# Output projection: sums of weights stand beside kept pieces of the first group, and transpositions move one piece back

## The chip, the cores and the metric

One core of a Trainium2 chip runs the whole program. The metric is the device time of one execution in microseconds (us). Three runs of the kernel before gave 922.68, 921.38 and 921.91 us, a median of 921.91 us. The profiled execution took 922.59 us by its own measurement, of which the profile's span covers 920.8 us.

## The reference, cut to what matters

Two layers act on a sequence of 256 rows of width 2048. Each layer projects its input, runs three groups of attention heads, gates their outputs, and maps the joined result through one output projection. A residual and a layer norm close the layer.

```
for l in range(DEPTH):                       # DEPTH = 2
    h = x @ w_in                             # x (256, 2048)
    ...
    mkv = mem @ w_mem_kv                     # memory keys and values, mem (256, 2048)
    ...
    y = concat([y_a * silu(a_z), y_b * silu(b_z), y_m * silu(m_z)])   # (256, 2048)
    out = y @ w_out                          # (256, 2048) x (2048, 2048)
    x = layer_norm(ALPHA * x + out, ln_g, ln_b)
```

The change is in `y @ w_out`, for columns 0 to 1023 of it, and in how the next layer's input is transposed after the layer norm.

## The kernel before, in words

**Pieces.** Weights come from memory as pieces of 512 KB (128 partitions x 1024 floats). `plan()` lists all of them in the order of use, and `take()` hands them out. For each piece SP issues a DMA into a tile `raw` (a ring of four). ACT casts it to a short-mantissa tile `wh` (L256, ring of four). DVE subtracts to get the rest `wl` (L263, ring of three). PE multiplies with both: an operand's high part with `wh`, its low part with `wh`, its high part with `wl`. `advance` keeps the high tile three pieces ahead and the low tile two ahead. PE and SP run in the order in which the program is written. DVE and ACT run in an order that a scheduler works out before the kernel is built, and each then works through its queue strictly in that order.

**The output projection.** Columns 0 to 1023 are two groups of 512 columns (n = 0 and n = 1), columns 1024 to 2047 are two more. The first two groups are computed by a Strassen-like scheme (`out_unit`, L872) for the first 3 (layer 0) or 2 (layer 1) of the four k-quarters of y, and plainly for the rest. The letters of `OUT_B` and `OUT_A` set the row of pieces:

- B, a plain block product of one quarter: 6 matmuls on 512 columns (`plain`, L882).
- K, a kept piece: the quarters that the scheme leaves out. A piece feeds both row tiles, t = 0 and 1, so 12 matmuls (`kept`, L898). Those of n = 1 come first, then those of n = 0.
- T, a sum of weight blocks, which DVE adds (L255) before ACT and DVE split it: 6 matmuls (`sums`, L912).
- O, a piece of the last two column groups, 12 matmuls (`others`, L1126). What the row leaves of them follows at its end.

A row is `OUT_B[l]`, then `OUT_A[l]`. With 3 O at the end of layer 0's row (one of `OUT_A`'s letters TO and two more) and 1 at the end of layer 1's, the last T stands three pieces and one piece before the end.

**Banks.** PSUM has eight banks, here 0 to 7. `pair()` alternates between banks 0-1 and 2-3 at each call; every stream of pieces that needs two banks calls it when it starts. Banks 4 to 7 serve the head generators, and then `out_unit`: before the change bank 7 collects (t 0, n 0), 6 (t 0, n 1), 5 (t 1, n 0) and 4 (t 1, n 1); when T starts, 7 and 6 are read into the residual (L913, L914) and used again for two of the four sums. After the last T eight DVE instructions (L922 to L929) combine the banks into the residual `res`, and three `bn_stats` (L931) follow.

**After the row.** In layer 0 the generator `norm_between` (L794) runs beside layer 1's first 16 pieces (the memory's keys and values, L965): one `tick()` per piece lets it go on. It aggregates the statistics (L799), takes the reciprocal root (L496 to L501, ACT's square root with a load of its table), normalises `res` in eight instructions (L804), and after `yield 3` transposes it in eight steps of four transpositions (L817) into banks 4 and 5 in turn, which ACT reads (L820). When the 16 pieces are done, the next stream of pieces (`ws_pieces(..., first=4)`, L1011) writes banks 4 and 5. In layer 1 eight closing pieces (`last3`, numbered 0 to 7 here) follow the row, the last five of which have tiles of their own (`room`, `w`). They run twice: for row tile 0 (L1141 on), then for row tile 1. Then comes the last norm.

Of the kernel before, what the change touches and what calls it, by code (L numbers as in the profile page):

```python
# [18 lines left out]
T = 256  # L19
# [9 lines left out]
PART_B = "WB" * 12  # L29
PART_A = "TW" * 16  # L30
QUARTERS = (3, 2)
OUT_B = ("BBOBBOBKBKBKBKB", "BBKBKBKBKBKKKK")
OUT_A = ("TO" * 12 + "OO", "TO" * 8)

G_MK, G_MV, G_BQK, G_AQ0, G_AK0, G_AQ1, G_AK1, G_MQ, G_BZ, G_AZ0, G_AZ1, G_MZ, G_WO = range(13)
HI_AHEAD, LO_AHEAD, RAWS = 3, 2, 4
# [16 lines left out]
def hybrid_trunk_kernel(  # L53
# [87 lines left out]
    def plan():  # L141
        for l in range(L):
            def keys(p):
                g = w512[l, G_MK].rearrange("(h q) p n -> q p h n", h=2)
                return Load(g[p // 2, :, :, p % 2 * 512:p % 2 * 512 + 512], (2, 512))

            def add_sums(b11, b12, b21, b22, n, beside):
                sums = []
                for q in range(len(b11)):
                    for k, d in enumerate(Load(None, (2, n)) for _ in range(4)):  # L150
                        d.sum = (q, k)
                        d.parts = [[(0, b11[q]), (1, b12[q])], [(2, b22[q])], [], [(3, b21[q])]][k]
                        sums.append(d)
                for d in sums:
                    d.at = len(loads)
                    if d.sum[0] and d.sum[1] < 2:
                        i = d.sum[0] * 4 - 4
                        d.behind = (sums[i + 2].at, sums[i + 1].at) if d.sum[1] == 0 else (sums[i + 3].at, sums[i + 2].at)
                    if d.sum[1] < 2:
                        early.append(d)  # L160
                    loads.extend((d, next(beside)))

            def group(g, kp, n):
                loads.extend(Load(g[i], (kp, n)) for i in range(16 // kp))

            for p in range(8):
                if p % 2 == 0:
                    loads.append(Load(memT[p // 2], (4, T), "res" if l == 0 else None, (memq[l], p // 2)))
                loads.append(Load(w512[l, G_MV, p], (2, 512)))
                if p:  # L170
                    loads.append(keys(p - 1))
            loads.append(keys(7))
            for p in range(8):
                if l == 0 and p < 4:
                    loads.append(Load(xT[p], (4, T), "res", (xq[l], p)))
                if p == 4:
                    break
                loads.append(Load(w512[l, G_BQK, p], (4, 256)))
            stream = iter([Load(w512[l, g, p], (4, 256)) for g in (G_BQK, G_AQ0, G_AK0, G_AQ1) for p in range(8)][4:])
            b11, b12, b21, b22 = ([w388[l, n, 2 * q + k] for q in range(4)] for k, n in ((0, 0), (0, 1), (1, 0), (1, 1)))  # L180
            plain = iter([Load(b, (2, 388)) for b in b11 + b22 + b21])
            loads.extend(next(stream if c == "W" else plain) for c in PART_B)
            add_sums(b11, b12, b21, b22, 388, stream)
            group(w388[l, 2], 2, 388)
            loads.extend(stream)
            group(w388[l, 3], 2, 388)
            for g in (G_AK1, G_MQ, G_BZ, G_AZ0, G_AZ1, G_MZ):
                loads.extend(Load(w512[l, g, p], (4, 256)) for p in range(8))
            u, kq = [w512[l, G_WO + n] for n in range(2)], QUARTERS[l]
            b11, b12, b21, b22 = ([u[n][2 * q + k] for q in range(kq)] for k, n in ((0, 0), (0, 1), (1, 0), (1, 1)))  # L190
            last3 = [w256[l].rearrange("h q p n -> q p h n")[p // 2, :, :, p % 2 * 512:p % 2 * 512 + 512] for p in range(8)]
            plain = iter([Load(b, (2, 512)) for b in b11 + b22 + b21])
            kept = iter([Load(u[n][p], (2, 512)) for n in (1, 0) for p in range(2 * kq, 8)])
            others = iter([Load(w512[l, G_WO + 2, p], (2, 512)) for p in range(8)] +
                          ([] if l == L - 1 else [Load(b, (2, 512)) for b in last3]))
            loads.extend(next(dict(B=plain, K=kept, O=others)[c]) for c in OUT_B[l])
            add_sums(b11, b12, b21, b22, 512, others)
            loads.extend(others)
            if l == L - 1:
                for p, b in enumerate(last3):  # L200
                    home = ("asv", "mk", "mv", "qk", "qk")[p - 3] if p >= 3 else None
                    loads.append(Load(b, (2, 512), home))
                    if home:
                        loads[-1].room = p
# [589 lines left out]
    def norm_between(l, x):  # L794

        mvt = small([P, 2, 2], "mvt")
        rstd = small([P, 2], "rstd")
        for t in range(2):
            dve.bn_aggr(mvt[:, t], stats[:, t, :4])  # L799
        rsqrt(rstd, mvt[:, :, 1], 2, LN_EPS)  # L800
        for q in range(4):
            for t in range(2):
                r = res[:, t, columns(q)]
                dve.tensor_scalar(r, r, mvt[:, t, 0:1], rstd[:, t:t + 1], op0=ALU.subtract, op1=ALU.mult)  # L804
            if q == 0:
                yield 2
        yield 3
        for q in range(4):
            o = operand()
            x.append(o)  # L810
            for j in range(0, 4, 2):
                pt, = yield from banks(1)
                z = gated()
                for jj in range(2):
                    kt = q * 4 + j + jj
                    for t in range(2):
                        pe.transpose(ps[:, pt, jj * T + t * P:jj * T + (t + 1) * P], res[:, t, kt * P:(kt + 1) * P], ident)  # L817
                for jj in range(2):
                    kt = q * 4 + j + jj
                    act.activation(z[:, jj], ps[:, pt, jj * T:(jj + 1) * T], AF.Identity, bias=lnt[:, 1, kt:kt + 1], scale=lnt[:, 0, kt:kt + 1])  # L820
                release(pt)
                parts(o[:, j:j + 2, 0], o[:, j:j + 2, 1], z)
                if j == 0:
                    z0 = z
                else:
                    x_differences(l, q, z0, z)
                yield 2 if (q, j) == (2, 2) else 1
# [44 lines left out]
    def out_unit(yq, ydiff, kq, rows):  # L872
        r11, r12, r21, r22 = (res[:, t, columns(n)] for t in range(2) for n in range(2))
        tmp = hd.tile([P, 512], F32, name=nm("tmp"), tag="term")
        open_ = set()

        def first(b):
# [3 lines left out]

        def plain():  # L882
            for q in range(kq):
                quarter(ps[:, 7], block(yq[q], 0, 0), first(7), False)
                if q == kq - 1:
                    act.copy(tmp, ps[:, 7])
                tick()
                yield
            for q in range(kq):
                quarter(ps[:, 6], ydiff[q][3], first(6), False)  # L890
                tick()
                yield
            for q in range(kq):
                quarter(ps[:, 7], block(yq[q], 0, 1), False, False)
                tick()
                yield

        def kept():  # L898
            for n in (1, 0):
                for p in range(2 * kq, 8):  # L900
                    w = take()
                    for kk in range(2):
                        kt = p * 2 + kk
                        for t, b in enumerate((7 - n, 5 - n)):
                            moving(ps[:, b], t, [v[:, kk] for v in w], yq[kt // 4], kt % 4, first(b), kt == 15)
                    if n and p == 7:
                        dve.scalar_tensor_tensor(r22, r22, ALPHA, ps[:, 4], op0=ALU.mult, op1=ALU.add)
                        open_.remove(4)
                    tick()
                    yield  # L910

        def sums():  # L912
            add_residual(0, columns(0), ps[:, 7], 0)  # L913
            dve.scalar_tensor_tensor(r12, r12, ALPHA, ps[:, 6], op0=ALU.mult, op1=ALU.add)  # L914
            open_.difference_update((6, 7))
            for q in range(kq):
                s1, s2, s3, s4 = ydiff[q]
                for b, a in ((4, s1), (6, s3), (7, s2), (5, block(yq[q], 1, 1))):
                    quarter(ps[:, b], a, first(b), q == kq - 1)
                    if q == kq - 1 and b == 5:  # L920
                        q5, q7, q6, q4 = (ps[:, b] for b in (4, 6, 7, 5))
                        dve.tensor_tensor(tmp, q6, tmp, op=ALU.subtract)  # L922
                        dve.scalar_tensor_tensor(r21, r21, ALPHA, tmp, op0=ALU.mult, op1=ALU.subtract)
                        dve.tensor_tensor(r21, r21, q7, op=ALU.add)
# [325 lines left out]
```

## Time and profile before

| | |
|---|---|
| median of 3 runs | 921.91 us (921.38 to 922.68) |
| profiled execution | 922.59 us, of which the span is 920.8 us |
| DVE busy | 720.0 us, 78% |
| ACT busy | 553.8 us, 60% |
| DMA | 196.21 MB, mean 213 GB/s |
| layer 0's row of the output projection | from 369.26 us to 452.44 us of the span |
| layer 1's row | ends, and the closing pieces begin, a little over 30 us before the span's end |

In rows of the timeline the columns are: start in us, duration in us, engine, line, operation, output<-input, shape, count, and in brackets the idle time before it with what ended that wait. Adjacent instructions of a kind are merged into one row. `PEld` is the loading of the stationary operand, which runs under the matmuls. Matmuls overlap, so the time of one is the distance between starts and not the duration shown.

### The profile page before, as it was taken

How to read it: one execution, taken by the hardware profiler on the slowest of the kernel's cores; microseconds unless marked ns; L12 is line 12 of the kernel's file. 1: busy time of each engine (PE TensorE's matmuls, PEld its weight loads, DVE VectorE, ACT ScalarE, POOL GpSimd, SP SyncE). 2: the span in 40 equal slices, each digit the busy share in tenths (PEclk: the TensorE clock that was granted, in tenths of full speed). 3: DMA queues.
4: the chain of work that ended last, by engine and by line, in shares of the span. 5: the costliest groups of instructions: out<-in, count | busy, mean ns of one | idle time of the engine just before them, and what ended most of it. 6: DMA issues, size and time to landing. Idle time of an engine off the chain costs nothing.

```text
span 920.8 us, 14554 instructions
## 1 busy us (share of the span) xinstructions
PE 908.2 (99%) x5480; PEld 795.6 (86%) x5480; DVE 720.0 (78%) x997; ACT 553.8 (60%) x809; POOL 13.5 (1%) x32
## 2 busy tenths in 40 slices
PE   8999999999999999999999999999999999999997
PEld 6889999998888888888878899999988888888875
DVE  6697788698665777799978768886877788777897
ACT  6565555676486766554568555557657676465550
POOL 1000000000000000000000000000000000100000
PEclk9999999999999999999999999999999999999998
DMA  8868786775444455886765687655644555868652
GB/s 300 279 204 275 253 282 204 235 242 177 158 138 160 161 177 189 300 271 221 232 209 173 200 293 252 224 192 175 225 159 137 196 175 179 288 214 294 215 173 92
DMA packets 65014, 196.21 MB, mean 213 GB/s; under 512 B 7088, under 2 KB 10288, under 8 KB 64944
## 3 DMA queue, kind: packets, MB, share of 16 engines
q1 hardware_dynamic: 63632, 192.55, 63.0%
q0 software_dynamic: 1024, 2.21, 0.7%
q8 instruction: 43, 0.70, 0.3%
q10 hardware_dynamic: 288, 0.52, 0.2%
q14 instruction: 27, 0.22, 0.1%
HBM read 193.16 MB, written 2.10 MB: 212 GB/s over the span
## 4 chain that ended last, share of the span: by engine, by line
PE 91%; DMA 3%; ACT 2%; DVE 2%; issue 1%; SPq 0%; ACTq 0%; DVEq 0%
PE ps L86 89%; DMA raw<-w 2%; DVE wl L263 1%; ACT wh L256 1%; PE ps L721 0%; DMA gws<-gate_w 0%; PE ps L817 0%; PE ps L759 0%; DVE w L263 0%; ACT sq L676 0%; SPq L344 0%; PE ps L688 0%; ACT sc L712 0%; SPq L339 0%; ACT res L861 0%
## 5 line engine op out<-in xcount | busy, mean ns | idle before, releaser
L263 DVE TENSOR_TENSOR wl<-raw,wh 128x1024 fp32r<-128x1024 f32 (+1 forms) x313 | 364.9, 1169 | 119.0 <-PE ps L86 59.8
L256 ACT CAST wh<-raw 128x1024 fp32r<-128x1024 f32 (+1 forms) x313 | 314.8, 1008 | 233.7 <-PE ps L86 130.8
L86 PE MATMUL ps<-x,wh 128*128 128x512 f32 x1408 | 446.4, 398 | 0.0
L86 PEld LDWEIGHTS ps<-x,wl 128*128 128x128 f32 x1408 | 265.1, 188 | 63.3 <-DVE wl L263 1.0
L86 PE MATMUL ps<-x,wl 128*128 128x256 f32 x1408 | 278.1, 279 | 0.3 <-DVE wl L263 0.3
L86 PE MATMUL ps<-wh,x 128*128 128x512 f32 (+1 forms) x852 | 246.3, 370 | 0.6 <-ACT wh L350 0.6
L86 PEld LDWEIGHTS ps<-x,wh 128*128 128x128 f32 x1408 | 219.6, 189 | 1.7 <-issue 0.3
L86 PEld LDWEIGHTS ps<-wh,x 128*128 128x128 f32 x852 | 155.0, 188 | 20.0 <-ACT wh L350 1.7
L86 PE MATMUL ps<-wl,x 128*128 128x512 f32 (+1 forms) x426 | 157.7, 370 | 0.0
L86 PEld LDWEIGHTS ps<-wl,x 128*128 128x128 f32 x426 | 80.0, 188 | 11.4 <-DVE wl L351 1.1
L256 ACT CAST wh<-term 128x776 fp32r<-128x776 f32 (+1 forms) x39 | 36.0, 923 | 49.4 <-DVE term L255 41.3
L263 DVE TENSOR_TENSOR wl<-term,wh 128x776 fp32r<-128x776 f32 (+1 forms) x39 | 41.5, 1065 | 16.6 <-PE ps L86 15.8
L255 DVE TENSOR_TENSOR term<-term,term 128x776 f32<-128x776 f32 (+1 forms) x39 | 41.3, 1060 | 0.7 <-DMA term<-w 0.7
L86 PE MATMUL ps<-wh,s 128*128 128x512 f32 (+1 forms) x144 | 41.2, 368 | 0.0
L86 PEld LDWEIGHTS ps<-wh,s 128*128 128x128 f32 x144 | 25.9, 188 | 3.2
L86 PE MATMUL ps<-wl,s 128*128 128x512 f32 (+1 forms) x72 | 26.6, 369 | 0.0
L712 ACT ACTIVATE sc<-sc,mx 128x128 f32<-128x128 f32 (+1 forms) x32 | 14.2, 444 | 7.5 <-DVE mx L710 7.4
L487 DVE SCALAR_TENSOR_TENSOR sz<-ps,sz 128x512 f32<-128x512 f32 x24 | 16.4, 686 | 2.8 <-ACT sz L486 2.1
L86 PE MATMUL ps<-wh,sc 128*128 128x388 f32 x64 | 16.5, 338 | 0.0
L86 PE MATMUL ps<-w,x 128*128 128x512 f32 (+1 forms) x72 | 15.0, 361 | 1.3 <-DVE w L263 1.2
L86 PEld LDWEIGHTS ps<-w,x 128*128 128x128 f32 x72 | 11.8, 189 | 4.4 <-DVE w L263 2.5
L491 DVE TENSOR_TENSOR s<-raw,s 128x512 fp32r<-128x512 f32 (+1 forms) x23 | 12.6, 569 | 3.1 <-ACT s L490 3.1
(221 smaller groups left out, 713.8 us busy)
## 6 DMA issues: line engine op xcount, KB each, us to landing
raw<-w SPq DMA_DIRECT2D x252, 512.0 KB, 4.3
raw<-w SPq DMA_DIRECT2D x64, 388.0 KB, 3.7
term<-w SPq DMA_DIRECT2D x24, 388.0 KB, 4.3
term<-w SPq DMA_DIRECT2D x15, 512.0 KB, 4.7
bias<-relw SPq DMA_DIRECT2D x16, 192.0 KB, 3.8
res<-xT SPq DMA_DIRECT2D x4, 512.0 KB, 6.3
res<-xn SPq DMA_DIRECT2D x4, 512.0 KB, 4.7
raw<-memT SPq DMA_DIRECT2D x4, 512.0 KB, 4.5
```

Of the source, the lines that this page charges most:

```text
L86: pe.matmul(o, l, r, start=start, stop=stop, skip_group_check=True)
L255: in_order(dve.tensor_tensor(d.raw, d.raw, d.plus, op=ALU.add))
L256: act.copy(d.hi, d.raw)
L263: in_order(dve.tensor_tensor(d.lo, d.raw, d.hi.bitcast(F32), op=ALU.subtract))
L487: dve.scalar_tensor_tensor(dst, a, scale, dst, op0=ALU.mult, op1=ALU.add)
L491: dve.tensor_tensor(lo, src, hi.bitcast(F32), op=ALU.subtract)
L712: act.activation(s[:, own[t]], s[:, own[t]], AF.Exp, bias=mx[:, t:t + 1], accum_out=zs[:, t:t + 1])
```

## The change

Three things change. First, the rows of letters: two K of layer 0 and four K of layer 1 (those of n = 0) move from `OUT_B` into `OUT_A`, beside T; as many O move to the row's end, so that 4 O (layer 0) and 5 O (layer 1) follow the last T. `add_sums` takes the row as a pattern for that. Second, the banks: (t 0, n 0) goes to a bank of its own, `x0`, and (t 1, n 1) to `x0 + 1`. They come from a further call of `pair()` ahead of O's own, so O of the same layer takes the other pair than before. Banks 4 and 7 are then untouched until T uses them. Third, `yield 3` before the transpositions becomes `yield 4`. The numbers of matmuls, sums and loads stay.

```diff
-OUT_B = ("BBOBBOBKBKBKBKB", "BBKBKBKBKBKKKK")
-OUT_A = ("TO" * 12 + "OO", "TO" * 8)
+OUT_B = ("BBOBBOBKBKBBOB", "BBKBKBKBKB")
+OUT_A = ("TKTK" + "TO" * 10 + "OOO", "TK" * 4 + "TO" * 4 + "OOOO")
...
-            def add_sums(b11, b12, b21, b22, n, beside):
+            def add_sums(b11, b12, b21, b22, n, pattern, beside):
...
-                for d in sums:
+                left = iter(sums)
+                for c in pattern:
+                    if c != "T":
+                        loads.append(next(beside[c]))
+                        continue
+                    d = next(left)
...
-                    loads.extend((d, next(beside)))
+                    loads.append(d)
...
-            add_sums(b11, b12, b21, b22, 388, stream)
+            add_sums(b11, b12, b21, b22, 388, PART_A, dict(W=stream))
...
-            loads.extend(next(dict(B=plain, K=kept, O=others)[c]) for c in OUT_B[l])
-            add_sums(b11, b12, b21, b22, 512, others)
-            loads.extend(others)
+            beside = dict(B=plain, K=kept, O=others)
+            loads.extend(next(beside[c]) for c in OUT_B[l])
+            add_sums(b11, b12, b21, b22, 512, OUT_A[l], beside)
...
-        yield 3
+        yield 4
...
         tmp = hd.tile([P, 512], F32, name=nm("tmp"), tag="term")
+        x0 = pair()
...
-                quarter(ps[:, 7], block(yq[q], 0, 0), first(7), False)
+                quarter(ps[:, x0], block(yq[q], 0, 0), first(x0), False)
...
-                        for t, b in enumerate((7 - n, 5 - n)):
+                        for t, b in enumerate((6, x0 + 1) if n else (x0, 5)):
...
-                    if n and p == 7:
-                        dve.scalar_tensor_tensor(r22, r22, ALPHA, ps[:, 4], op0=ALU.mult, op1=ALU.add)
-                        open_.remove(4)
+                    if p == 7 and n:
+                        dve.scalar_tensor_tensor(r22, r22, ALPHA, ps[:, x0 + 1], op0=ALU.mult, op1=ALU.add)
+                    elif p == 7:
+                        add_residual(0, columns(0), ps[:, x0], 0)
...
         def sums():
-            add_residual(0, columns(0), ps[:, 7], 0)
             dve.scalar_tensor_tensor(r12, r12, ALPHA, ps[:, 6], op0=ALU.mult, op1=ALU.add)
-            open_.difference_update((6, 7))
+            open_.remove(6)
...
-                for b, a in ((4, s1), (6, s3), (7, s2), (5, block(yq[q], 1, 1))):
+                for b, a in ((4, s1), (7, s3), (6, s2), (5, block(yq[q], 1, 1))):
```

How the order moves, at three places. Lines of the changed kernel are 5 or 6 higher than those of before. Numbers in names tell tiles apart.

**First place.** PE at layer 0's first O piece (operand `x_2901`, weights `wh_3711`, `wl_3743`), the third piece of the row, with what a row waits for, before:

```order
L86 MATMUL ps<-wl_3713,x_3654 128x512
L86 MATMUL ps<-wh_3711,x_2901 128x512 [waits Activation_49]
L86 MATMUL ps<-wh_3711,x_2901 128x512
L86 MATMUL ps<-wl_3743,x_2901 128x512 [waits DVE_49]
L86 MATMUL ps<-wh_3711,x_2901 128x512 x2
```

And in the changed kernel:

```order
L86 MATMUL ps<-wl_3713,x_3654 128x512
L86 MATMUL ps<-wh_3711,x_2901 128x512 [waits DVE_49]
L86 MATMUL ps<-wh_3711,x_2901 128x512
L86 MATMUL ps<-wl_3743,x_2901 128x512
L86 MATMUL ps<-wh_3711,x_2901 128x512 x2
```

The O piece's first matmul waited for ACT's cast, and its third for DVE's rest. It now waits for DVE at the first, and that covers the third: O writes the pair of banks that the last gate product filled, which DVE reads in L487 behind the rests of two pieces.

**Second place.** ACT in layer 1, at the readings of the last two steps of transpositions (rows with `sz<-ps,lnt`), just before the stream of pieces that writes banks 4 and 5; `wh_4859` is the cast of that stream's third piece, `mv` that of the memory's values, `s` and `sc` those of differences that DVE makes. Before:

```order
L256 CAST wh_4837<-raw_4748 128x1024
L490 CAST sc_4725<-raw_4727 128x256
L490 CAST mv_4384<-ps 128x1024
L490 CAST sc_4726<-raw_4727 128x256
L820 ACTIVATE sz_4785<-ps,lnt 128x256 x2
L490 CAST s_762_4724<-raw_4727 128x512
L820 ACTIVATE sz_4814<-ps,lnt 128x256 x2
L256 CAST wh_4859<-raw_4766 128x1024
```

In the changed kernel:

```order
L495 CAST sc_4749<-raw_4751 128x256
L495 CAST sc_4750<-raw_4751 128x256
L261 CAST wh_4814<-raw_4725 128x1024
L495 CAST mv_4384<-ps 128x1024
L825 ACTIVATE sz_4805<-ps,lnt 128x256 x2
L495 CAST s_768_4748<-raw_4751 128x512
L495 CAST x_4804<-sz_4805 128x2x256
L261 CAST wh_4859<-raw_4766 128x1024
L825 ACTIVATE sz_4836<-ps,lnt 128x256 x2
```

The last reading stood ahead of the cast `wh_4859` and stands behind it and behind the cast `x_4804` now.

**Third place.** DVE at the end of layer 1's row; `wl_8555` and `wl_8575` are the rests of closing pieces 1 and 2, `w_...` those of the pieces from 3 on. Before:

```order
L263 TENSOR_TENSOR wl_8555<-raw_8479,wh_8528 128x1024
L925 TENSOR_TENSOR res<-res,ps 128x512
L927 TENSOR_TENSOR res<-res,tmp_8086 128x512
L928 TENSOR_TENSOR res<-res,tmp_8086 128x512
L781 SCALAR_TENSOR_TENSOR res<-res,ps 128x512
L263 TENSOR_TENSOR wl_8575<-raw_8497,wh_8553 128x1024
L263 TENSOR_TENSOR w_8573<-room_8499,w_8573 128x1024
L781 SCALAR_TENSOR_TENSOR res<-res,ps 128x512
L263 TENSOR_TENSOR w_8584<-room_8499,w_8583 128x1024
L931 BN_STATS stats<-res 128x6 x2
L929 TENSOR_TENSOR res<-res,ps 128x512
L263 TENSOR_TENSOR w_8594<-raw_8502,w_8593 128x1024
```

In the changed kernel, where `wl_8496` and `wl_8519` belong to the last two O pieces and `wl_8537` to closing piece 0:

```order
L931 TENSOR_TENSOR res<-res,ps 128x512
L933 TENSOR_TENSOR res<-res,tmp_8092 128x512
L934 TENSOR_TENSOR res<-res,tmp_8092 128x512
L268 TENSOR_TENSOR wl_8496<-raw_8425,wh_8476 128x1024
L937 BN_STATS stats<-res 128x6 x2
L935 TENSOR_TENSOR res<-res,ps 128x512
L268 TENSOR_TENSOR wl_8519<-raw_8437,wh_8494 128x1024
L939 TENSOR_TENSOR res<-res,sc_8073 128x512
L937 BN_STATS stats<-res 128x6
L268 TENSOR_TENSOR wl_8537<-raw_8455,wh_8517 128x1024
L939 TENSOR_TENSOR res<-res,sc_8077 128x512
L268 TENSOR_TENSOR wl_8555<-raw_8480,wh_8535 128x1024
```

The steps that close the scheme stood among the rests of the closing pieces 1 to 5, and stand ahead of closing piece 1 now. ACT's casts there, before:

```order
L256 CAST wh_8510<-raw_8450 128x1024
L256 CAST wh_8528<-raw_8479 128x1024
L256 CAST wh_8553<-raw_8497 128x1024
L256 CAST w_8573<-room_8499 128x1024
L256 CAST w_8583<-room_8499 128x1024
```

In the changed kernel:

```order
L261 CAST wh_8517<-raw_8455 128x1024
L261 CAST wh_8535<-raw_8480 128x1024
L261 CAST w_8573<-room_8500 128x1024
L261 CAST wh_8553<-raw_8498 128x1024
L261 CAST w_8583<-room_8500 128x1024
```

The cast of closing piece 3 (`w_8573`) has come ahead of that of piece 2 (`wh_8553`).

More of the change, by code (lines that the diff above doesn't have):

```diff
@@ L883, in plain @@
             for q in range(kq):
-                quarter(ps[:, 7], block(yq[q], 0, 0), first(7), False)
+                quarter(ps[:, x0], block(yq[q], 0, 0), first(x0), False)
                 if q == kq - 1:
-                    act.copy(tmp, ps[:, 7])
+                    act.copy(tmp, ps[:, x0])
                 tick()
@@ L893, in plain @@
             for q in range(kq):
-                quarter(ps[:, 7], block(yq[q], 0, 1), False, False)
+                quarter(ps[:, x0], block(yq[q], 0, 1), False, False)
                 tick()
@@ L912, in sums @@
         def sums():
-            add_residual(0, columns(0), ps[:, 7], 0)
             dve.scalar_tensor_tensor(r12, r12, ALPHA, ps[:, 6], op0=ALU.mult, op1=ALU.add)
-            open_.difference_update((6, 7))
+            open_.remove(6)
             for q in range(kq):
                 s1, s2, s3, s4 = ydiff[q]
-                for b, a in ((4, s1), (6, s3), (7, s2), (5, block(yq[q], 1, 1))):
+                for b, a in ((4, s1), (7, s3), (6, s2), (5, block(yq[q], 1, 1))):
                     quarter(ps[:, b], a, first(b), q == kq - 1)
                     if q == kq - 1 and b == 5:
-                        q5, q7, q6, q4 = (ps[:, b] for b in (4, 6, 7, 5))
+                        q5, q7, q6, q4 = (ps[:, b] for b in (4, 7, 6, 5))
                         dve.tensor_tensor(tmp, q6, tmp, op=ALU.subtract)
```

## The prediction

> **What bounds the kernel now.** I began with the page: the busy times of the engines.
>
> ```profile
> span 920.8 us, 14554 instructions
> PE 908.2 (99%) x5480; PEld 795.6 (86%) x5480; DVE 720.0 (78%) x997; ACT 553.8 (60%) x809; POOL 13.5 (1%) x32
> ```
>
> PE is busy for all but 12.6 us of 920.8, and the change leaves the number of matmuls alone. So a gain can only come out of PE's idle time and out of matmuls that run slower than they need to. The next view is PE's timeline, for the pace of an undisturbed stretch.
>
> ```profile
> 397.90 0.62 PE L86 MATMUL ps<-wh,s 128*128 128x512 f32 x2
> ...
> 457.88 0.62 PE L86 MATMUL ps<-x,wh 128*128 128x512 f32 x2
> ```
>
> Between these starts lie 59.98 us and 264 matmuls on 512 columns: 0.227 us each. So a B or T piece takes 6 x 0.227 = 1.36 us, a K or O piece 2.72 us. Whatever takes longer is loss. I then walked PE's timeline through the places that the diff touches: layer 0's row, layer 1's first pieces (the transpositions), and layer 1's row with the closing pieces. Two of them show loss. The first is the boundary between the layers:
>
> ```profile
> 468.66 0.39 PE L86 MATMUL ps<-wl,x 128*128 128x512 f32 x1
> 470.71 1.00 PE L817 MATMUL ps<-ident,res 128*128 128x128 f32 x4 [1.66 <-DVE res L804]
> ...
> 475.90 0.60 PE L817 MATMUL ps<-ident,res 128*128 128x128 f32 x4
> 476.26 0.72 PE L86 MATMUL ps<-wh,x 128*128 128x512 f32 x2
> ...
> 479.13 0.60 PE L817 MATMUL ps<-ident,res 128*128 128x128 f32 x4
> 479.48 0.71 PE L86 MATMUL ps<-x,wh 128*128 128x512 f32 x2
> ```
>
> PE stood for 1.66 us before the first transposition step. The piece behind it started at 471.47 and took until 475.90, against 479.13 - 476.26 = 2.87 us for the next one. The windows say why (us, PE busy, granted clock, DMA share, GB/s):
>
> ```profile
> 473.00:474.00 1.00, 1.00 (x5) 0.50 0.03 12
> 474.00:475.00 1.00, 1.00 (x5) 0.50 0.00 0
> 476.00:477.00 1.00, 1.00 (x8) 1.00 0.68 188
> ```
>
> After the idle time PE was granted half its clock for some 3 us. The second place is the closing pieces of row tile 0:
>
> ```profile
> 888.14 0.61 PE L86 MATMUL ps<-wh,x 128*128 128x512 f32 x2
> ...
> 889.77 3.51 PE L86 MATMUL ps<-w,x 128*128 128x512 f32 x14
> 894.53 4.29 PE L86 MATMUL ps<-w,x 128*128 128x512 f32 x16 [1.25 <-DVE w L263]
> ...
> 902.74 7.22 PE L86 MATMUL ps<-w,x 128*128 128x512 f32 x42
> ```
>
> From 888.14 to 902.74 run 54 matmuls in 14.60 us; at 0.227 they take 12.26. The loss is 2.3 us, half of it the wait of 1.25 for a rest of DVE.
>
> **The change, part by part.** Durations are those of the profiled execution, 922.59 us, which lies 0.7 above the median of 921.91; the sum is made against it.
>
> *Transpositions one piece later.* The end of the normalisation sets when the first step may start:
>
> ```profile
> 461.15 0.26 DVE L799 BATCH_NORM_AGGREGATE mvt<-stats 128x2 f32<-128x24 f32 x1
> 468.59 1.22 DVE L263 TENSOR_TENSOR wl<-raw,wh 128x1024 fp32r<-128x1024 f32 x1 [1.26 <-ACT wh L256]
> 470.11 3.74 DVE L804 TENSOR_SCALAR res<-res,mvt,rstd 128x512 f32<-128x512 f32 x8
> ```
>
> The statistics were aggregated at 461.15, but the eight normalisations came at 470.11, behind a rest that had itself waited. A block takes 3.74 / 8 = 0.47 us, so the first is ready at 470.6. After the change PE runs one more memory piece before the first step: 468.89 (its last matmul's start at 468.66 and 0.23) + 2.8 = 471.7. Even with DVE's chain unmoved the wait is gone, with 1 us to spare, and with it the cause of the half clock. And the chain should come earlier, since the scheme's last combinations are now done before layer 0's last four pieces rather than three. From the end of the piece at 468.89 to the start of the next memory piece but one at 476.26 the trace has 7.37 us; undisturbed it is a step (479.48 - 479.13 = 0.35), a piece (2.88) and a step, 3.59. The term is **-3.8 us**. What is late next is the other end of the transpositions, below.
>
> [...]
>
> *O takes the other pair of banks.* Layer 0's first O writes the pair of the last gate product:
>
> ```profile
> 370.23 0.60 ACT L486 ACTIVATE sz<-ps 128x512 f32<-128x512 f32 x1
> 372.01 0.61 PE L86 MATMUL ps<-wh,x 128*128 128x512 f32 x2
> 372.05 0.69 DVE L487 SCALAR_TENSOR_TENSOR sz<-ps,sz 128x512 f32<-128x512 f32 x1
> ```
>
> The matmul at 372.01 began while DVE was just starting its read of that pair. It must now wait until the read is done: 372.74 - 372.01 = **+0.7 us**. Bounds 0.4 (if DVE takes the read a little sooner, the O piece being one that needs its rest later) and 0.9 (if it starts 0.2 later). PE loses it whole, as every matmul behind it is in order. Layer 1 has no O before its first T, so it isn't paid there.
>
> *The last transposition step and the banks 4 and 5.* The stream behind the memory pieces writes these banks. It began at 504.21, two memory pieces behind the last step; after the change only one lies between. What must fit in it is ACT's reading of the last step:
>
> ```profile
> 498.20 0.60 PE L817 MATMUL ps<-ident,res 128*128 128x128 f32 x4
> 498.56 0.71 PE L86 MATMUL ps<-x,wh 128*128 128x512 f32 x2
> ...
> 504.21 0.63 PE L86 MATMUL ps<-x,wh 128*128 128x512 f32 x2
> ```
>
> ```profile
> 490.76 1.05 ACT L256 CAST wh<-raw 128x1024 fp32r<-128x1024 f32 x1 [3.02 <-DMA raw<-w]
> ...
> 499.60 1.02 ACT L490 CAST mv<-ps 128x1024 fp32r<-128x1024 f32 x1
> ...
> 500.81 1.03 ACT L820 ACTIVATE sz<-ps,lnt 128x256 f32<-128x256 f32 x2
> 501.72 0.63 ACT L490 CAST s<-raw 128x512 fp32r<-128x512 f32 x1
> 502.23 1.04 ACT L820 ACTIVATE sz<-ps,lnt 128x256 f32<-128x256 f32 x2
> 503.14 1.07 ACT L256 CAST wh<-raw 128x1024 fp32r<-128x1024 f32 x1
> ```
>
> The step ended at 498.56 and its reading at 503.27: 4.7 us later, with 5.65 of cover. In the new order the reading stands behind one more cast of 1024 columns and one of an operand. Walk ACT's queue from the end of memory piece 13, which was 498.20 here: the `mv` cast starts 1.40 later, takes 0.90 to the next, the second last reading 0.91, `s` 0.51, the operand 0.52, `wh` 0.95, the last reading 1.04; together 6.23. With the small `sc` cast (0.31) and a DVE step for the operand (0.4) it is 6.9. PE is there after a step, a piece, a step and a piece: 0.35 + 2.88 + 0.35 + 2.79 = 6.37. That leaves 0.6; the walk counts no idle time of ACT, so I take **+0.8 us**. The low bound is 0: ACT's lag goes back to its wait of 3.02 us for a load, and that need not recur. The high bound takes the old lag whole: 4.7 + 0.95 - 2.83 = 2.8. I stay near the low end because the queue's rows, added up, lie there.
>
> *The closing pieces.* The losses from 888 to 903 come from this order on DVE and ACT:
>
> ```profile
> 884.38 1.05 ACT L256 CAST wh<-raw 128x1024 fp32r<-128x1024 f32 x1 [2.01 <-DMA raw<-w]
> 885.63 1.05 ACT L256 CAST w<-room 128x1024 fp32r<-128x1024 f32 x1 [0.20 <-DMA room<-w]
> ...
> 892.67 0.67 DVE L929 TENSOR_TENSOR res<-res,ps 128x512 f32<-128x512 f32 x1
> 893.25 1.22 DVE L263 TENSOR_TENSOR w<-raw,w 128x1024 fp32r<-128x1024 f32 x1
> ```
>
> The rest that PE waited for at 894.53 ran at 893.25 behind the scheme's last combinations. With five O behind the last T these are over before closing piece 1, so DVE's part of the loss goes. What remains is ACT, which takes its casts as loads land, and piece 3's now stands ahead of piece 2's: if that load is late, piece 2 waits. A whole recovery is -2.3; losing 1.3 more than that leaves -1.0. I take **-1.6 us**, the middle, as neither end has a nearer row.
>
> *Kept pieces beside sums, in both rows.* A sum costs DVE an addition and a rest:
>
> ```profile
> 418.56 1.22 DVE L263 TENSOR_TENSOR wl<-term,wh 128x1024 fp32r<-128x1024 f32 x1 [0.58 <-PE ps L86]
> ```
>
> DVE waits here 0.58 us per T and wide piece, on PE, so it keeps up with a wide piece beside each T; K and O are equally wide, so T beside K costs PE nothing. Before T, B and O now alternate where B and K did: also the same widths. The reads of the first banks (0.7 us of DVE in the place of the same read elsewhere) fit into that slack; uncovered they would cost up to 0.7 each. **0**.
>
> Sum: -3.8 + 0.7 + 0.8 - 1.6 = -3.9, so 918.7 for an execution like the profiled one, and 918.0 for the median.
>
> **The rivals.** *All covered.* The bank wait vanishes, the first O's is at its low bound, and the tail comes back whole: -3.8 + 0.4 - 2.3 = -5.7, 916.3. For it speaks the load wait of 3.02 that need not recur; against it that the first O's wait shows in the rows almost by itself.
>
> *The tail is not recovered.* The inverted casts cost what DVE gives back: -3.8 + 0.7 + 0.8 = -2.3, 919.6. For it: the casts at 884.38 and 885.63 both waited for loads. Against: more lead from five O.
>
> *The wait moves to the banks, and with it the half clock.* The reading has its old lag, PE waits 2.8 in the place of 0.8, and then runs at half clock, which cost 7.37 - 3.59 - 1.66 = 2.1 at the boundary: -3.9 + 2.0 + 2.1 = +0.2, 922.1. For it: 1.66 of waiting had this effect at 470.71. Against: a wait of 1.25 at 894.53 had not, by the pace of the 16 matmuls behind it (4.13 us for 16, 0.26 each, not 0.45). [...]
>
> *Slower.* ACT may lag more than at the last step. At the sixth step it did:
>
> ```profile
> 488.81 0.60 PE L817 MATMUL ps<-ident,res 128*128 128x128 f32 x4
> ...
> 495.98 1.01 ACT L820 ACTIVATE sz<-ps,lnt 128x256 f32<-128x256 f32 x2
> ```
>
> The step ended at 489.16 and its reading at 496.99, 7.8 later, after that load came late. With this lag the bank wait is 7.8 - 2.9 = 4.9, and 0.95 for the cast now ahead, 5.9 in the place of 0.8, and 2.1 of half clock: -3.9 + 5.1 + 2.1 = +3.3, 925.2. It turns the sign when the bank wait passes 2.6: 3.9 + 0.8 = 4.7 are saved without it, less 2.1 for the clock. For it: loads near 490 are late already. Against: six us of queue lie between, in which ACT caught up to 4.7.
>
> *The change doesn't do what it says.* The waiting goes, but the half clock stays, because something other than the wait brought it about: -3.9 + 2.1 = -1.8, 920.1. For it: a wait of 1.25 did not halve the pace. Against: the clock is 1.00 again a few us later, and no other loss lies near.
>
> **How the numbers follow.** Times of rivals are against the median, 921.9. Forecast (916.6 to 919.6) 0.57; all covered 0.12; tail not recovered 0.08; half clock stays 0.04; bank wait with half clock 0.12; slower 0.07. A measurement of this kernel tells about 0.2%, 1.8 us, from no change: faster means under 920.07, slower over 923.75. So faster is 0.57 + 0.12 + 0.08 = 0.77, same 0.04 + 0.12 = 0.16, slower 0.07. The range runs from 915.6 (all covered, and the first O's wait gone too, with 0.3 left for rows that I cost at nothing) to 922.1 (bank wait at its upper bound, with half clock); beyond it lie the slower case and some 0.08 of the ends.
>
> **What would show it.** No idle time before the first transposition and a granted clock of 1.00 through 480; the memory piece behind it at 2.88. A wait for DVE of 0.4 to 0.9 at the first O near 372. A wait for ACT of 0 to 2.8 before the stream behind the memory pieces, near 500. From closing piece 2 to the run of 42 matmuls 12.3 to 13.6 us in the place of 14.60, with the wait, if any, on ACT. Wrong it would be if the clock dropped at a new place, if T beside K left PE waiting for DVE in the rows, or if more than 3 us were lost at banks 4 and 5.

## The result and the profile after

The changed kernel takes 919.28 us (median of 7 runs, 918.70 to 921.25); the kernel before, in 7 runs beside it, 922.68. The ratio is 0.9964, with a 95% interval of 0.9952 to 0.9976: faster by 0.36%, clear of no change. The forecast was 918.0 against 921.9, 0.42%. The profiled execution took 919.35 us by its own measurement.

The page of the changed kernel, its span and its busy times:

```profile
span 917.5 us, 14547 instructions
PE 906.5 (99%) x5480; PEld 795.1 (87%) x5480; DVE 718.8 (78%) x997; ACT 553.0 (60%) x809; POOL 13.5 (1%) x32
```

PE is still the bound, with the same 5480 matmuls, and its idle time has gone from 12.6 to 11.0 us. The rest of the 3.3 us is matmuls that no longer run slowly. Next is the view that sums PE's waits (us in total, times, longest), whole lines of the changed kernel:

```profile
PE ps L86 <- ACT sz L825: 1.1, 1, 1.1
PE ps L86 <- DVE sz L492: 0.6, 1, 0.6
PE ps L86 <- DVE wl L268: 0.6, 2, 0.4
```

The two largest waits of before that the change touches, 1.7 for `res` and 1.2 for `w`, are not in this list any more. Two others are new: 1.1 for ACT's reading (`sz`, L825) and 0.6 for DVE's read of the gate's banks (`sz`, L492). PE's timeline of the changed kernel shows where they are, from the row's first O over the boundary and the banks 4 and 5 to the closing pieces:

```profile
372.85 0.73 PE L86 MATMUL ps<-wh,x 128*128 128x512 f32 x2 [0.61 <-DVE sz L492]
...
472.64 0.60 PE L822 MATMUL ps<-ident,res 128*128 128x128 f32 x4
473.00 0.71 PE L86 MATMUL ps<-wh,x 128*128 128x512 f32 x2
473.89 0.50 PE L86 MATMUL ps<-wl,x 128*128 128x512 f32 x1 [0.18 <-DVE wl L268]
...
476.27 0.60 PE L822 MATMUL ps<-ident,res 128*128 128x128 f32 x4
...
501.62 0.39 PE L86 MATMUL ps<-x,wh 128*128 128x512 f32 x1
503.12 0.50 PE L86 MATMUL ps<-x,wh 128*128 128x512 f32 x1 [1.11 <-ACT sz L825]
...
887.04 0.62 PE L86 MATMUL ps<-wh,x 128*128 128x512 f32 x2
...
888.40 7.09 PE L86 MATMUL ps<-w,x 128*128 128x512 f32 x30
...
899.41 7.21 PE L86 MATMUL ps<-w,x 128*128 128x512 f32 x42
```

The first transposition step (472.64) follows its piece with no wait. The 30 matmuls of the closing pieces stand in one row: no wait parts them. One small loss was not foreseen: the piece at 473.00 took 3.27 us until 476.27, 0.40 more than the 2.87 of its like, with a wait for a rest in it. The granted clock stays whole there (windows of the changed kernel: us, PE busy, granted clock, DMA share, GB/s):

```profile
473.00:474.00 1.00, 0.82 (x6) 1.00 0.88 317
474.00:475.00 1.00, 1.00 (x5) 1.00 0.28 84
```

DVE's timeline of the changed kernel shows why the boundary is free:

```profile
459.42 0.24 DVE L804 BATCH_NORM_AGGREGATE mvt<-stats 128x2 f32<-128x24 f32 x1
466.69 1.46 DVE L809 TENSOR_SCALAR res<-res,mvt,rstd 128x512 f32<-128x512 f32 x3
468.07 1.22 DVE L268 TENSOR_TENSOR wl<-raw,wh 128x1024 fp32r<-128x1024 f32 x1
```

The first normalisations came at 466.69 (470.11 before) and were done by 468.15. PE ended the sixth memory piece, behind which the first step stood before the change, at 469.87. So the new rows alone might have cleared the boundary, and the later place of the transpositions might only have cost the new wait at the banks. That is what the first experiments ask.

### The profile page after: what moved, and what is told of

The parts are those of the page before. It is cut to its first block, busy times and chain, and to the rows that moved or that the text cites. A ratio compares the mean times of both kernels' runs of the same rounds, so it can differ in the third digit from the quotient of the medians.

```text
span 917.5 us, 14547 instructions
## 1 busy us (share of the span) xinstructions
PE 906.5 (99%) x5480; PEld 795.1 (87%) x5480; DVE 718.8 (78%) x997; ACT 553.0 (60%) x809; POOL 13.5 (1%) x32
## 5 line engine op out<-in xcount | busy, mean ns | idle before, releaser
L492 DVE SCALAR_TENSOR_TENSOR sz<-ps,sz 128x512 f32<-128x512 f32 x24 | 16.3, 683 | 1.6 <-ACT sz L491 1.0
L86 PEld LDWEIGHTS ps<-wl,s 128*128 128x128 f32 x72 | 13.5, 188 | 1.6
L1104 ACT ACTIVATE sz<-sz 128x512 f32<-128x512 f32 x16 | 10.1, 632 | 8.0 <-DVE sz L492 7.9
L495 ACT CAST s<-raw 128x512 fp32r<-128x512 f32 (+1 forms) x23 | 11.3, 524 | 5.8 <-DVE raw L409 5.8
```

Of the source, the lines that this page charges most:

```text
L86: pe.matmul(o, l, r, start=start, stop=stop, skip_group_check=True)
L492: dve.scalar_tensor_tensor(dst, a, scale, dst, op0=ALU.mult, op1=ALU.add)
L495: act.copy(hi, src)
L1104: act.activation(sz, sz, AF.Silu)
```

## The experiments

Each is the changed or the old kernel with the edit shown. Ratios are against the kernel before, with their 95% intervals.

**Transpositions back at their old place**, rows and banks as changed:

```diff
-        yield 4
+        yield 3
```

> The changed kernel with the transpositions back at their old place (yield 3); rows and banks stay as changed. Theory A (the rows alone clear the boundary): in the changed kernel DVE had finished the first three normalisations at 468.07, before PE ended the memory piece at 469.87 behind which the old place lies. So no idle time before the first transposition, the granted clock stays 1.00 there, and the wait of 1.11 us before the stream on banks 4 and 5 goes, as two pieces lie behind the last step again: about 1.2 us less than the changed kernel, 918.1. Theory B (the later place carries the gain): DVE's order follows the place, the normalisations come late again, PE waits 1 to 2 us and gets half the clock: 2 to 3.5 us more than the changed kernel, 921.3 to 922.8.

Measured: 917.89 us, ratio 0.9935 (0.9919 to 0.9952), 1.4 less than the changed kernel. PE's timeline of this kernel:

```profile
469.97 0.60 PE L822 MATMUL ps<-ident,res 128*128 128x128 f32 x4
473.22 0.60 PE L822 MATMUL ps<-ident,res 128*128 128x128 f32 x4
476.41 0.60 PE L822 MATMUL ps<-ident,res 128*128 128x128 f32 x4
```

No row carries a wait, and the steps are a piece and a step apart (3.25, 3.19), so the clock is whole. The wait near 500 is gone as well. Theory A holds: with the new rows, the later place only costs.

**The later place alone**, in the kernel before:

```diff
-        yield 3
+        yield 4
```

> The kernel before with the transpositions one piece later (yield 4) and nothing else; rows and banks as before. Theory A and B alike: the first transposition has no wait (its blocks were ready at about 471, PE needs it at 471.7), which brings about 3.5 us; the stream on banks 4 and 5 waits about 1.3 us for ACT as in the changed kernel; layer 0's first O has no wait; the closing pieces keep their loss, 14.6 us from closing piece 2 to the run of 42 matmuls. Sum -3.5 + 1.3 = -2.2: 920.5. Rival: with the chain of before the normalisations slip behind one more rest, the wait stays at 1 us or more and the clock with it: 922 or more.

Measured: 920.04 us, ratio 0.9960 (0.9945 to 0.9976). With the old rows the later place clears the boundary too; no wait stands before the first step at 472.86. But the banks cost less than expected, as PE's timeline of this kernel shows:

```profile
498.18 0.60 PE L817 MATMUL ps<-ident,res 128*128 128x128 f32 x4
...
501.41 0.85 PE L86 MATMUL ps<-x,wh 128*128 128x512 f32 x2
502.10 0.40 PE L86 MATMUL ps<-x,wl 128*128 128x256 f32 x2
```

From the first pair of that stream to the next row are 0.69 us where 0.46 is usual: 0.2 lost, not 1.3. ACT read the last step at 500.66 here and at 502.04 in the changed kernel, with the step at nearly the same time (498.18 and 498.39). The cover of one piece is therefore nearly enough; the rest of the 1.27 of the changed kernel comes from what ACT has ahead of that reading. The closing pieces kept their wait of 1.25.

**Layer 0's first O one piece later:**

```diff
-OUT_B = ("BBOBBOBKBKBBOB", "BBKBKBKBKB")
+OUT_B = ("BBBOBOBKBKBBOB", "BBKBKBKBKB")
```

> The changed kernel, with layer 0's first O one B piece later (BBBOBO in the place of BBOBBO). Theory: the wait of 0.61 us that the profile shows before this O (0.77 by starts) is the read of the gate's banks and nothing else; the O starts 1.36 us later and finds the banks read. No wait there, 0.6 to 0.8 us less than the changed kernel, 918.6, all of it visible at the end of layer 0's row. Rival: the next O follows its neighbour closer, and a weight piece or its rest comes late in its place; the row ends as late as in the changed kernel.

Measured: 917.68 us, ratio 0.9930 (0.9911 to 0.9949), 1.6 less than the changed kernel. Not all of it is the wait. From the row's start to the third memory piece of layer 1 PE takes 88.62 us before (369.26 to 457.88), 89.52 in the changed kernel (369.33 to 458.85) and 88.62 here (368.95 to 457.57): the edit brings 0.9. Another 0.4 of this trace lies ahead of the row, where the programs are alike, and is no gain of the edit.

**Layer 1's old row:**

```diff
-OUT_B = ("BBOBBOBKBKBBOB", "BBKBKBKBKB")
-OUT_A = ("TKTK" + "TO" * 10 + "OOO", "TK" * 4 + "TO" * 4 + "OOOO")
+OUT_B = ("BBOBBOBKBKBBOB", "BBKBKBKBKBKKKK")
+OUT_A = ("TKTK" + "TO" * 10 + "OOO", "TO" * 8)
```

> The changed kernel with layer 1's row of letters as before (all kept pieces ahead of T, one O behind the last T). Theory: the closing pieces lose 2.2 us again, 14.4 to 14.6 us from closing piece 2 to the run of 42 matmuls, with DVE as the one waited for; everything ahead of the row is as in the changed kernel: 2.2 us more, 921.5. Rival: the loss came from the loads and the order of ACT's casts, and stays gone by half or more: 920.4 or less.

Measured: 921.44 us, ratio 0.9979 (0.9966 to 0.9993), 2.2 more than the changed kernel. PE's timeline of this kernel has the old picture back:

```profile
887.20 0.61 PE L86 MATMUL ps<-wh,x 128*128 128x512 f32 x2
...
888.85 3.48 PE L86 MATMUL ps<-w,x 128*128 128x512 f32 x14
893.58 4.29 PE L86 MATMUL ps<-w,x 128*128 128x512 f32 x16 [1.26 <-DVE w L268]
...
901.79 7.21 PE L86 MATMUL ps<-w,x 128*128 128x512 f32 x42
```

From the first of these rows, where closing piece 2 begins, to the last are 14.59 us, against 899.41 - 887.04 = 12.37 in the changed kernel and 14.60 before. The closing pieces' gain belongs to layer 1's row, whole.

**Both repairs together** (the old place, and the first O one piece later, as in the two diffs above):

> The changed kernel with both repairs: transpositions at the old place (yield 3) and layer 0's first O one B piece later. Theory: the two waits are independent, so the gains add. The old place brought 1.4 us in the medians and 1.6 in the spans (919.28 to 917.89, 917.5 to 915.9), the later O 0.9 us by the starts in layer 0's row. Against the kernel with the old place alone 0.9 less: 917.0, a span of about 915.0, with no wait of PE for DVE near 372, none before the first transposition, none near 500. Rival: the row's chain on DVE changes with the O, the normalisations slip behind the old place, and a wait of 0.5 us or more stands before the first transposition: 917.9 or more.

Measured: 916.92 us, ratio 0.9935 (0.9923 to 0.9947), with a span of 914.5, against 0.9964 for the changed kernel. This beats both kernels. That the two gains add up is shown by the traces (a span of 914.5 against 915.9 with the old place alone) and not by the ratios: those of the two single repairs, 0.9935 and 0.9930, are not told apart from this one. The list of PE's waits of this kernel, down to 0.5, has nothing left from the places of the change (the rest waited for, `wl`, belongs to the kernel's first pieces, at 13.68):

```profile
PE ps L86 <- DVE wh L325: 1.5, 1, 1.5
PE ps L726 <- ACT yr L596: 0.8, 1, 0.8
PE ps L86 <- DVE wl L268: 0.5, 1, 0.5
PE ps L726 <- DVE sc L721: 0.5, 1, 0.5
```

**Layer 0's old row with the old place:**

```diff
-OUT_B = ("BBOBBOBKBKBBOB", "BBKBKBKBKB")
-OUT_A = ("TKTK" + "TO" * 10 + "OOO", "TK" * 4 + "TO" * 4 + "OOOO")
+OUT_B = ("BBOBBOBKBKBKBKB", "BBKBKBKBKB")
+OUT_A = ("TO" * 12 + "OO", "TK" * 4 + "TO" * 4 + "OOOO")
-        yield 4
+        yield 3
```

> The changed kernel with the old place (yield 3) and layer 0's old row of letters (three O behind the last T); banks and layer 1's row as changed. Theory: what makes the normalisations early is layer 0's row (a fourth O behind the last T, so that the combinations are done one piece earlier). With the old row the first normalisation comes at 470 again, PE waits 1.3 to 1.9 us before the first transposition and gets half the clock: 3.5 to 4.2 us more than with the new row and the old place (917.9), so 921.4 to 922.1, and the first O keeps its wait of 0.6. Rival: the separate bank, not the row, shortens the chain (its read into the residual stands elsewhere), the normalisations are ready by 468.5 and there is no wait: 917.9, within 0.7.

Measured: 922.44 us, ratio 1.0005 (0.9992 to 1.0018). The time hit the theory's range for a reason that it did not have. The old letters end with a B behind the last K. With the new banks that B writes the first bank when it has been read already, so its product is left out of the result, and it has to wait for the read. PE's timeline of this kernel:

```profile
400.80 0.70 PE L86 MATMUL ps<-wh,x 128*128 128x512 f32 x2 [1.87 <-DVE res L786]
...
476.05 1.00 PE L822 MATMUL ps<-ident,res 128*128 128x128 f32 x4 [0.99 <-DVE res L809]
```

Its windows behind the first of these rows have half the clock:

```profile
401.00:402.00 1.00, 1.00 (x5) 0.83 0.12 49
402.00:403.00 1.00, 1.00 (x4) 0.50 0.11 33
...
405.00:406.00 1.00, 1.00 (x6) 0.97 0.00 0
```

Most of the loss in this trace lies at 400, in the wait and the slow stretch. The profiled execution took 924.78, 2.3 more than the median, so the trace shows more of the loss than the median has. At the boundary a wait is back, of 0.99 only, without loss of clock. The run does not separate the two theories well, so it was made again without that B.

**The same with the last K behind the last B:**

```diff
-OUT_B = ("BBOBBOBKBKBKBKB", "BBKBKBKBKB")
+OUT_B = ("BBOBBOBKBKBKBBK", "BBKBKBKBKB")
```

> The changed kernel with the old place (yield 3) and three O behind the last T of layer 0, kept pieces all ahead of T, but with the last K behind the last B (BBK at the end of the first part in the place of BKB), so that the first bank is read only when it is complete and no piece waits for that read. Theory (layer 0's row makes the normalisations early): no wait of 1.9 us within the row near 400, as that one came from a B behind the read; a wait of 0.9 to 1.8 us before the first transposition. Below some 1.5 us the clock stays, 918.9 to 919.3, beyond it falls to half and the time is 921 to 922. Rival (the separate bank makes them early): no wait there, 917.9 within 0.5.

Measured: 921.29 us, ratio 0.9985 (0.9976 to 0.9995), 3.4 more than with the new row and the same place. PE's and DVE's timelines of this kernel:

```profile
471.12 1.01 PE L822 MATMUL ps<-ident,res 128*128 128x128 f32 x4 [1.33 <-DVE res L809]
...
495.63 0.65 PE L822 MATMUL ps<-ident,res 128*128 128x128 f32 x4 [1.85 <-ACT sz L825]
```

```profile
461.88 0.25 DVE L804 BATCH_NORM_AGGREGATE mvt<-stats 128x2 f32<-128x24 f32 x1
470.51 3.75 DVE L809 TENSOR_SCALAR res<-res,mvt,rstd 128x512 f32<-128x512 f32 x8
```

With three O behind the last T the statistics are ready at 461.88, and the normalisations come at 470.51; with the new row and the same place (the first experiment) these are 459.52 and 466.60. So layer 0's row makes them early, the bank does not. The clock stayed whole behind the first wait, and the boundary alone costs 1.33 and 0.4 more inside the step. Those 0.4 are no slow matmuls: the second transposition reads row tile 1's block, whose normalisation ends 0.47 behind the first, and PE stands idle from 471.45 to 471.55. The other half of the 3.4 is a second wait, 1.85 at a later step whose bank ACT had not read. ACT's timeline shows what stood straight ahead of that reading, a weight cast that had itself waited for PE:

```profile
493.62 1.04 ACT L261 CAST wh<-raw 128x1024 fp32r<-128x1024 f32 x1 [2.10 <-PE ps L86]
```

Its wait of 3.04 us for a load, as in the profile of before, ended earlier, at 489.85. The time fell into the range that was named for half the clock, but by this second wait; for a whole clock 918.9 to 919.3 was expected.

**Transpositions two and three pieces earlier than changed** (`yield 2` and `yield 1` in the place of `yield 4`):

> The changed kernel with the transpositions two pieces earlier than it has them (yield 2). The first blocks are normalised at 467.7 by its trace, PE is there at 467.1. Theory (a wait at this place costs its own length, and half the clock only beyond some 1.3 to 1.7 us): a wait of 0.4 to 1.2 us, a granted clock of 1.00 behind it: 918.4 to 919.1, that is 0.5 to 1.2 more than with yield 3. Rival (any wait at this place brings the half clock, as the place decides and not the length): 2 us more on top, 920.4 to 921.1, with 0.50 in the windows behind it.

> The changed kernel with the transpositions three pieces earlier (yield 1). PE is there at 464.4 and the first blocks are normalised at 467.7 by the changed kernel's trace. Theory (beyond some 1.7 us the half clock costs a fixed 2 us or so, whatever the length): a wait of 3.0 to 3.8 us, then half clock for 3 to 3.5 us, 5 to 6 us more than with yield 3: 922.9 to 923.9. Rival (the slow stretch grows with the wait): half clock for twice as long, about 4 us lost to it: 925 or more. If DVE's order follows the place, the normalisations come earlier and the wait is shorter; the windows then still show how long the clock was half for the wait there was.

Measured: 919.67 us, ratio 0.9964 (0.9951 to 0.9977), and 921.93, ratio 0.9992 (0.9981 to 1.0004). With `yield 2` there is no recorded wait before the first step, the clock is whole, and its four transpositions took 0.67 instead of 0.35, again with a short wait for the second block inside the step (PE is busy for 0.02 us of the 0.1 from 467.4). The larger loss is elsewhere: two later steps waited 0.46 and 0.83 us for ACT's reading. The time is 0.6 above the expected range, and the place of the loss was not foreseen. With `yield 1`, PE's timeline of that kernel shows

```profile
465.39 1.00 PE L822 MATMUL ps<-ident,res 128*128 128x128 f32 x4 [1.41 <-DVE res L809]
```

and not 3 us or more: DVE's order followed the place, and the normalisations came at 464.79. Behind 1.41 us the clock stayed at 1.00, so neither theory on the clock was put to the test by it. Its profiled execution (920.6) is at the fast end of its runs (920.4 to 923.9), so the trace shows less of the loss than the median has.

**The kernel before with the transpositions one piece earlier**, for a longer wait (`yield 2` in the place of `yield 3`), **and the kernel before once more:**

> The kernel before with the transpositions one piece earlier (yield 2). PE is at the first one at about 466.1, and by the trace of before its blocks are ready at 470.6; DVE's order may bring them to 469. Theory (a wait beyond 1.66 us gives half the clock for about 3 us, whatever its length): a wait of 3 to 4.6 us, windows at 0.50 for about 3 us behind it, 1.4 to 2.9 us more than before: 924.1 to 925.6. Rival (the slow stretch grows with the wait): 0.50 for 5 us or more and 1 us more on top, above 926.5.

> The kernel before once more, for a second trace of it. If the half clock follows from the wait before the first transposition, this trace shows the same wait (1.4 to 1.9 us) and 0.50 behind it again. If it depends on the moment and not on the wait, the same wait stands there with 1.00 behind it, and the execution is about 2 us shorter.

Measured: 924.74 us, ratio 1.0021 (1.0008 to 1.0034), and 923.86 in a single execution. The longer wait, with windows behind it, in the first of the two:

```profile
469.90 1.36 PE L817 MATMUL ps<-ident,res 128*128 128x128 f32 x4 [3.37 <-DVE res L804]
```

```profile
469.00:470.00 1.00, 0.10 (x1) 0.98 0.85 307
470.00:471.00 1.00, 1.00 (x5) 0.50 0.95 201
...
473.00:474.00 1.00, 1.00 (x5) 0.81 0.01 4
```

Twice the wait of before (1.66), the same slow stretch: 0.50 for 3.42 us by these windows, against 3.41 in the first trace of before (last section). The second trace of before repeats its first, with a somewhat longer wait:

```profile
471.26 1.01 PE L817 MATMUL ps<-ident,res 128*128 128x128 f32 x4 [2.01 <-DVE res L804]
```

```profile
472.00:473.00 1.00, 1.00 (x8) 0.95 0.97 377
473.00:474.00 1.00, 1.00 (x4) 0.50 0.17 66
...
476.00:477.00 1.00, 1.00 (x8) 0.85 0.44 66
```

## Why the prediction was right

The sum was -3.9 us for the profiled execution; its span went from 920.8 to 917.5, -3.3. Each step was right in sign and place, and the sizes were off as follows.

- **The boundary, -3.8.** With the old place and the new rows (first experiment) the stretch from the end of the sixth memory piece to the piece behind the third step takes 476.76 - 469.97 = 6.79 us, against 479.48 - 468.89 = 10.59 before: -3.80, the number of the prediction. In the changed kernel that piece starts at 476.62, with one step fewer behind the end of the sixth piece at 469.87: 6.75 + 0.35 = 7.10, -3.5, chiefly since 0.40 goes to the slow piece at 473.00 that the prediction did not have. "And the chain should come earlier" was right and more than that: it makes the later place needless. The prediction gave the gain to the later place, which suffices too (the second experiment); what it did not ask is whether the rows alone suffice. Both traces of before have the half clock that makes up 2.1 us of this term; that a wait of this length brings it every time is not shown (last section).
- **The first O, +0.7.** From the row's start to the O's 3.52 - 2.75 = 0.77, and 0.90 over the row. The experiment that moves the O takes all of it away.
- **The banks 4 and 5, +0.8.** Measured 503.12 - 501.62 - 0.23 = 1.27, inside the bounds of 0 to 2.8. The step that was mis-sized is "the `mv` cast starts 1.40 later". ACT's timeline of the changed kernel:

```profile
497.30 1.05 ACT L261 CAST wh<-raw 128x1024 fp32r<-128x1024 f32 x1
498.25 1.00 ACT L495 CAST mv<-ps 128x1024 fp32r<-128x1024 f32 x1
...
502.04 1.03 ACT L825 ACTIVATE sz<-ps,lnt 128x256 f32<-128x256 f32 x2
503.10 0.62 ACT L495 CAST x<-sz 128x512 fp32r<-128x512 f32 x1
```

  The memory piece 13 ended at 495.16, so the `mv` cast started 3.09 behind it, with a weight cast straight ahead of it. From there to the end of the reading are 4.82 us, and the walk had 6.23 - 1.40 = 4.83. The walk was right from its second step on; its start was taken from a trace in which the queue ahead was another one. It hid part of this by adding 0.7 for casts that the queue then took in its stride.
- **The closing pieces, -1.6.** Measured: 899.41 - 887.04 = 12.37 against 14.60, -2.23, almost the whole recovery of -2.3. The cast of closing piece 3 ahead of that of piece 2 cost nothing: piece 2's cast began at 884.29 and PE came to it at 887.04. "The middle, as neither end has a nearer row" was the wrong choice: nothing had to be taken off. Whether the five O at the row's end or the K beside T bring the lead, no run separates.
- **Kept pieces beside sums, 0.** From the second matmul of the stream behind the memory pieces to closing piece 2, with layer 1's row in between, PE takes 888.14 - 504.45 = 383.69 us before and 887.04 - 503.12 = 383.92 in the changed kernel: 0.2 at most. Layer 0's row has 0.13 beside the first O's wait. Added up, the measured terms are -3.5 + 0.9 + 1.3 - 2.2 + 0.2 = -3.3, the span's change.
- **T beside K, 0.** No wait for DVE stands in either row behind the first O.
- **Of the rivals,** "all covered" fell with the two new waits (its sum gives 916.2 and not 916.3), "the tail is not recovered" with the 12.37 us, and the half clock that stays with the 1.00 behind the first transpositions. The slower one did not come, but its mechanism exists: ACT read a step late enough to hold PE for 1.85 us in one experiment, behind a cast that had waited for PE. The bank wait with half the clock did not come either: 1.11 us of waiting left the clock whole.

## What to carry to other kernels

When two edits of one change aim at the same wait, ask of each whether it removes the wait alone; here each did, and the second one only moved work towards the next deadline. Where a chain is made shorter, give it back the old place before a later one is chosen. A queue's walk is only as good as its first entry: take that entry from the new order, not from the old time of the same instruction.

## What the runs showed of the hardware

Whether the clock falls after a wait of PE does not follow from the length of the wait alone. Waits of 1.11 us (changed kernel), 1.25 (before, at 894.53), 1.33 and 1.41 left it at 1.00. Waits of 1.66, 1.87, 2.01 and 3.37 us were followed by 0.50. But the wait of 1.85 us at 495.63 (seventh step, layer 0's old row with the last K behind the last B) was not; the windows of that kernel read:

```profile
496.00:497.00 1.00, 1.00 (x7) 1.00 0.10 37
497.00:498.00 1.00, 1.00 (x6) 1.00 0.00 0
```

What parts 1.85 from 1.87 is not shown. Short windows of the kernel before show when its clock changed, since a mean of 0.86 or 0.57 tells how much of the 0.1 us ran at 0.50:

```profile
472.30:472.40 0.10, 0.10 (x2) 0.86 0.72 287
475.70:475.80 0.10, 0.10 (x3) 0.57 0.00 0
916.10:916.20 0.10, 0.00 (x0) 0.53 0.00 0
```

It fell at 472.37, rose at 475.78 and fell for the end of the program at 916.10. The slow stretch is 3.41 us. In the three other traces with a slow stretch the windows of 1 us at its two ends tell the same to about 0.02 us: a mean of 0.83 from 401.00, for one, puts the fall at 401.66, 0.86 behind the end of the wait at 400.80.

| Wait of PE, us | From its end to the fall of the clock, us | At 0.50, us |
|---|---|---|
| 3.37 (before, `yield 2`) | 0.06 | 3.42 |
| 2.01 (second trace of before) | 1.64 | 3.40 |
| 1.87 (layer 0's old row, at 400) | 0.86 | 3.40 |
| 1.85 (last K behind the last B) | no fall | 0 |
| 1.66 (before) | 1.66 | 3.41 |
| 1.41 (`yield 1`) | no fall | 0 |
| 1.33 (last K behind the last B, first step) | no fall | 0 |

In these four traces the length of the slow stretch did not follow the wait: 3.40 to 3.42 us for waits of 1.66 to 3.37. The fall came 0.06 to 1.66 us behind the end of the wait, and in no order of the waits' lengths. The table was made after the runs and none of them was made to test it. What happens between 1.41 and 1.66 us was not measured behind the first 10 us of a trace, and idle time is not all that goes with a fall: the last one in the kernel before came at 916.10, 0.15 us behind the end of PE's last matmul (915.95). In the 3 us before that end PE had stood idle once, for 0.34 us before 913.97, and had run, among others, matmuls of another shape (2x512).
